# A two-layer hybrid encoder on one core: order of projection units, scan parts and embedding units

## The chip, the cores and the metric

The kernel runs on one core of a Trainium2 chip. A core has a matrix engine (PE, TensorE; PEld is its weight load), a vector engine (DVE, VectorE), a scalar engine (ACT, ScalarE), a third elementwise engine (POOL, GpSimd) and a sequencer that issues transfers (SP, SyncE). They run side by side and meet at semaphores. The metric is the device time of one execution in microseconds (us); lower is better.

## The reference, cut to what matters

Tokens: 512; model width: 1024; two layers; all in float32. A layer, cut from the reference:

```python
u = _rmsnorm(h, norm_mix_g[l])
(s_z, s_xbc, s_dt, g_q, g_f, g_i, g_g, m_q, m_k, m_v, m_i, m_f, m_o,
 gates) = _split(u @ w_in[l], IN_SIZES)
y_ssd = _ssd_branch(s_z, s_xbc, s_dt, ...)        # conv, SSD scan in two directions, gate, group norm
y_hg = _hgrn2_branch(g_q, g_f, g_i, g_g, ...)     # gated linear scan, 8 heads
y_ml = _mlstm_branch(m_q, m_k, m_v, m_i, m_f, m_o, ...)
merged = (gate[:, :, 0] * (y_ssd @ w_br_ssd[l]) + gate[:, :, 1] * (y_hg @ w_br_hg[l])
          + gate[:, :, 2] * (y_ml @ w_br_ml[l]))
h = h + merged @ w_out[l]
u = _rmsnorm(h, norm_ffn_g[l])
up = _dwconv(u @ w_up[l], ffn_conv_w[l], ffn_conv_b[l])
h = h + (jax.nn.silu(a_half) * v_half) @ w_down[l]
h = h + (p[l] @ w_ple[l]) * jax.nn.sigmoid(h @ w_ple_gate[l])
```

A last RMS norm closes the trunk.

## The kernel before, in words

**Units.** Activations lie with channels on the 128 partitions and the 512 tokens along the free axis, so `h` is eight tiles of 128x512. A weight matrix is cut into units of 128 output columns. `weights` (line 192) loads a unit (512 KB, `wraw`) by a transfer on SP's queue and splits it into a rounded high part (`whi`, a cast on ACT) and the rest (`wlo`, a subtraction on DVE); three buffers of each. `proj` (line 214) multiplies: for each of eight slices k of the inner dimension three matmuls (high by high, high by low, low by high) into one PSUM bank. So a unit is 24 matmuls of 512 columns. The four banks of `pbank` are for projections, the four of `bank` for everything else. Nearly every tile of 128x512 comes from one pool with the tag `t2` and 36 buffers (line 1170).

**Norms.** `ssq_add` squares a tile of `h` on ACT and adds it to a running sum on POOL, or on DVE at the program's begin; the last square isn't added, except at the begin. `ssq_end` sums over partitions by small matmuls (`ssq`), `rstd` makes the reciprocal root on DVE and POOL, `ssq_bcast` spreads it by matmuls (`rb`). `norm_split` (line 298) then makes, for each of eight tiles, `u` on DVE, its high part `uh` on ACT and its low part `ul` on DVE. No projection of the next stage can begin before the first `uh`.

**Scans as jobs.** The scans are generators. At each `yield vec, lat` a job says how much DVE time its last part takes and what latency follows; the planner adds that to its own count of DVE time (`self.vec`) and sets the job's `ready`. `tick`, called after each k of a projection, resumes every job whose `ready` has passed in the planner's count of PE time (`self.now`); `finish` resumes without waiting. The planner's numbers only decide the order in which instructions are written down. PE's order is kept in the mixer (`manual_schedule` with PE, line 1005); the other engines' order comes from the framework's scheduler, by priority (`high_priority`).

**The mixer's order.** `ORDER` (line 20) is a list of steps: `a` and `b` are units of the SSD branch's groups 0 and 1 (four `xs`, then `sB`, `sC`), `z` a gate unit, `S` the start of the scalar work `scalars_ssd` (line 308), `0` and `1` the starts of the two SSD scans, `g` and `h` merge-gate units. Behind each `xs` unit `ssd_x` (line 559) makes the five-tap convolution (one ACT operation, four DVE operations) and the activation, giving `xc`, yields, and then has PE transpose `xc` into `tp` (line 189). Then come eight HGRN2 heads. `hg_proj(h)` (line 693) issues the units gq, gf0, gf1, for even heads the value units gv of two heads, and gg; then `finish(hg[h-1])` ends the scan of the head before, and the scan of head h starts. So the scan of an even head lies beside the units of an odd one (gq, gf0, gf1, gg) and the scan of an odd head beside those of an even one, which has the two value units besides. The last part of a head's scan makes the states `hst` and multiplies them into `hpo`; `hg_tail` normalises. `scalars_ml` (line 397) prepares the mLSTM scalars and starts with transposes into `rowp`.

**Begin and norms.** `begin` (line 505) projects the first three units (s0, 64 columns; xs0, xs1) from the tokens before the norm's factor is known, and scales the results afterwards: the s0 unit takes each tile of tokens as it arrives, xs0 and xs1 follow. Behind the norms stand embedding units (`ple_proj`, four pieces of six matmuls each for half of `p[l] @ w_ple[l]`): in layer 0 both halves stand behind the feed-forward norm, layer 1's halves behind the norm at the end of layer 0 and behind its own feed-forward norm. The feed-forward block (`ffn`, line 1093) takes its units `ua`, `uv` in turn.

Of the kernel before, what the change touches and what calls it, by code (L numbers as in the profile page):

```python
# [4 lines left out]
F32 = mybir.dt.float32  # L5
# [14 lines left out]
ORDER = "a a a a a z z a b S z z b 0 b b b b 1 z z z z g g g g g g g g h h h h h h h h"  # L20
# [100 lines left out]
class Body:  # L121
# [81 lines left out]

    def weights_split(self, raw):
# [9 lines left out]
    def proj(self, w, xh, xl, name, c0=0):  # L214
# [4 lines left out]
        for k in range(nk):  # L219
# [4 lines left out]
            if self.jobs:  # L224
                self.tick()
        return ps
# [22 lines left out]
    def ssq_add(self, q, x, later=False):  # L249
# [3 lines left out]
        q["i"] += 1  # L253
        last = q["i"] == q["n"] and not later
# [38 lines left out]

    def norm_apply(self, h, rb, g):
        with self.tc.high_priority(offset=NPRI):
            self.norm_split(h, rb, g)

    def norm_split(self, h, rb, g):
# [3 lines left out]
        for i in range(8):  # L302
            u = self.t2("u")
            nc.vector.scalar_tensor_tensor(u, h[i], self.pc(g, i), rb, op0=ALU.mult, op1=ALU.mult)
            self.split(u, self.uh[i], self.ul[i])


    def scalars_ssd(self):
# [4 lines left out]
        p4 = ps[:, 0:256].rearrange("p (t c) -> p t c", t=4)  # L313
        for t in range(4):
            nc.tensor.transpose(p4[:, t, :], raw[:, t * C:t * C + C], self.c("ident")[0:64, 0:64])
        rw = lambda n: self.rowt[:, ROW[n][0]:ROW[n][0] + ROW[n][1]].unsqueeze(1).to_broadcast([128, 4, ROW[n][1]])
        x = sm.tile([128, 4, 48], F32, name="spx")
        ii = sm.tile([128, 4, 16], F32, name="ii")
        nc.vector.tensor_tensor(x[:, :, 0:32], p4[:, :, 0:32], rw("dtb"), op=ALU.add)
        nc.vector.tensor_tensor(ii, p4[:, :, 32:48], rw("ib"), op=ALU.add)  # L320
        nc.vector.scalar_tensor_tensor(x[:, :, 32:48], p4[:, :, 48:64], -1.0, rw("fb"),
                                       op0=ALU.mult, op1=ALU.subtract)

        fl = lambda t: t.rearrange("p a b -> p (a b)")
        xf = fl(x)
        e = sm.tile([128, 192], F32, name="spe")
        nc.vector.scalar_tensor_tensor(e, xf, -1.0, xf, op0=ALU.mult, op1=ALU.min)
        nc.scalar.activation(e, e, AF.Exp)
        r = sm.tile([128, 192], F32, name="spr")
        nc.vector.tensor_scalar_add(r, e, 2.0)  # L330
        nc.vector.reciprocal(r, r)
        nc.vector.tensor_tensor(r, r, e, op=ALU.mult)
        q = sm.tile([128, 192], F32, name="spq")
        nc.vector.tensor_tensor(q, r, r, op=ALU.mult)
        nc.vector.tensor_scalar_mul(e, q, 2.0 / 17)
        for n in (15, 13, 11, 9, 7, 5, 3):
            nc.vector.scalar_tensor_tensor(e, e, 2.0 / n, q, op0=ALU.add, op1=ALU.mult)
        nc.vector.scalar_tensor_tensor(e, e, 2.0, r, op0=ALU.add, op1=ALU.mult)
        sp = sm.tile([128, 4, 48], F32, name="sp")
        nc.vector.scalar_tensor_tensor(fl(sp), xf, 0.0, e, op0=ALU.max, op1=ALU.add)  # L340
        self.dt = sp[:, :, 0:32]
        a = sm.tile([128, 32], F32, name="acoef")
        nc.scalar.activation(a, self.rowt[:, ROW["alog"][0]:ROW["alog"][0] + 32], AF.Exp)
        la = sm.tile([128, 4, 48], F32, name="la")
        nc.vector.scalar_tensor_tensor(la[:, :, 0:32], self.dt, -1.0,
                                       a.unsqueeze(1).to_broadcast([128, 4, 32]),
                                       op0=ALU.mult, op1=ALU.mult)
        nc.vector.tensor_scalar_mul(la[:, :, 32:48], sp[:, :, 32:48], -1.0)
# [919 lines left out]
```

## Time and profile before

| | |
|---|---|
| median of three runs | 2979.97 us (2977.85 to 2980.33) |
| the profiled execution | 2980.76 us, of which the span is 2978.9 us |
| PE busy | 2896.2 us, 97% of the span |
| DVE, ACT, POOL busy | 1865.3, 1185.4, 270.6 us |
| mean share of the TensorE clock that was granted | 0.987 |

The page shows PE busy in nearly every slice of the span, and of the transfers a mean of 98 GB/s. The time between the span and the profiled execution's own time, 1.9 us, lies outside the program's instructions. Views used below: the waits (who waited for whom), the stretches (busy time of each engine between two points, with the granted clock, called PEclk, 1.00 being full speed), the timeline (instructions in order of time; in brackets how long the engine had been idle and what ended that), and the groups of instructions.

### The profile page before, as it was taken

The page shows a single profiled execution, that of the slowest core. Times are in us where ns is not written, and L with a number is a line of the kernel's source. Part 1 is how long each engine was busy: PE and PEld are TensorE (multiplying, and loading weights), DVE is VectorE, ACT ScalarE, POOL GpSimd, SP SyncE. Part 2 cuts the span into 40 slices and gives each one's busy share as a digit, 9 for nine tenths or more (in the row PEclk, how much of TensorE's full clock was granted, in tenths as well). Part 3 has the DMA queues.
Part 4 walks back from the last instruction along what each step waited for, and adds up shares of the span by engine and source line. Part 5 has one row for each costly group of instructions (what it writes and reads, how often), then busy time and mean ns, then how long its engine had stood idle before and what let it go on. Part 6 is the DMA issues. An engine that isn't in the chain of part 4 may idle for free. (4 is left out here: it accounts for less than half of the span.)

```text
span 2978.9 us, 40295 instructions
## 1 busy us (share of the span) xinstructions
PE 2896.2 (97%) x15998; PEld 2412.1 (81%) x15998; DVE 1865.3 (63%) x3194; ACT 1185.4 (40%) x2018; POOL 270.6 (9%) x209
## 2 busy tenths in 40 slices
PE   7999999999999999999989999999999999999998
PEld 6777788888888888888867787888888888888887
DVE  6776767776565455546458768668765654555454
ACT  5443544553233343334344425455532323433342
POOL 0132100001100110000101321000010001000001
PEclk9999999999999999999999999999999999999999
DMA  3443222223322333333424331221232224332332
GB/s 129 114 128 115 71 72 78 72 72 110 103 85 85 134 114 99 98 94 102 153 90 124 117 114 60 83 72 64 72 121 92 86 92 135 101 98 96 97 101 95
DMA packets 120459, 293.34 MB, mean 98 GB/s; under 512 B 10608, under 2 KB 43760, under 8 KB 120272
## 3 DMA queue, kind: packets, MB, share of 16 engines
q1 hardware_dynamic: 120272, 290.79, 30.4%
q8 instruction: 125, 2.05, 0.3%
q14 instruction: 62, 0.51, 0.1%
HBM read 277.97 MB, written 12.78 MB: 98 GB/s over the span
## 5 line engine op out<-in xcount | busy, mean ns | idle before, releaser
L236 DVE TENSOR_TENSOR wlo<-wraw,whi 128x1024 fp32r<-128x1024 f32 (+2 forms) x454 | 575.2, 1268 | 483.5 <-ACT whi L235 481.0
L235 ACT CAST whi<-wraw 128x1024 fp32r<-128x1024 f32 (+2 forms) x454 | 472.4, 1041 | 895.8 <-issue 146.3
L155 PE MATMUL ga<-uh,whi 128*128 128x512 f32 x384 | 161.2, 420 | 0.0
L155 PE MATMUL pbr<-yh,whi 128*128 128x512 f32 x384 | 153.7, 400 | 0.0
L155 PE MATMUL ga<-uh,wlo 128*128 128x512 f32 x384 | 151.4, 394 | 0.0
L155 PE MATMUL ga<-ul,whi 128*128 128x512 f32 x384 | 150.9, 393 | 0.0
L155 PE MATMUL pbr<-yh,wlo 128*128 128x512 f32 x384 | 150.9, 393 | 0.0
L155 PE MATMUL pbr<-yl,whi 128*128 128x512 f32 x384 | 150.7, 392 | 0.0
L155 PE MATMUL ua<-uh,whi 128*128 128x512 f32 x352 | 137.4, 390 | 3.6 <-ACT uh L235 3.6
L155 PE MATMUL pdn<-sl,whi 128*128 128x512 f32 x352 | 137.4, 390 | 0.0
L155 PE MATMUL pdn<-sh,wlo 128*128 128x512 f32 x352 | 137.2, 390 | 0.0
L155 PE MATMUL ua<-uh,wlo 128*128 128x512 f32 x352 | 137.1, 390 | 0.0
L155 PE MATMUL uv<-uh,whi 128*128 128x512 f32 x352 | 137.1, 390 | 0.0
L155 PE MATMUL uv<-ul,whi 128*128 128x512 f32 x352 | 137.1, 390 | 0.0
L155 PE MATMUL uv<-uh,wlo 128*128 128x512 f32 x352 | 137.1, 390 | 0.0
L155 PE MATMUL pdn<-sh,whi 128*128 128x512 f32 x352 | 136.8, 391 | 0.0
L155 PE MATMUL ua<-ul,whi 128*128 128x512 f32 x352 | 136.8, 390 | 0.0
L258 POOL TENSOR_TENSOR sq<-sq 128x512 f32<-128x512 f32 x36 | 53.0, 1473 | 899.2 <-issue 767.5
L287 POOL TENSOR_TENSOR rs<-ms,mhalf 128x4 f32<-128x4 f32 x41 | 44.7, 1091 | 917.1 <-DVE ms L285 917.1
L774 ACT COPY hqc<-hQ 128x512 f32<-128x512 f32 x96 | 64.4, 671 | 114.8 <-DVE hQ L785 48.1
L155 PE MATMUL gf<-uh,whi 128*128 128x512 f32 x256 | 104.3, 407 | 0.0
L1107 DVE TENSOR_TENSOR h<-h,pdn 128x512 f32<-128x512 f32 x48 | 33.0, 688 | 111.8 <-PE pdn L155 111.8
(409 smaller groups left out, 7508.0 us busy)
## 6 DMA issues: line engine op xcount, KB each, us to landing
wraw<-wf SPq DMA_DIRECT2D x420, 512.0 KB, 3.6
att<-acd SPq DMA_DIRECT2D x32, 512.0 KB, 7.2
wraw<-wf SPq DMA_DIRECT2D x32, 448.0 KB, 3.3
me<-rtd SPq DMA_DIRECT2D x32, 256.0 KB, 4.3
h<-xT SPq DMA_DIRECT2D x16, 256.0 KB, 4.6
gad<-gth SPq DMA_DIRECT2D x16, 256.0 KB, 2.0
gdr<-gad SPq DMA_DIRECT2D x16, 256.0 KB, 5.4
ppd<-pp SPq DMA_DIRECT2D x16, 256.0 KB, 2.1
```

The lines of the kernel that those rows point to most:

```text
L155: return self.nc.tensor.matmul(out, lhsT, rhs, **k)
L235: nc.scalar.copy(hi, src)
L236: nc.vector.tensor_tensor(lo, src, hi.bitcast(F32), op=ALU.subtract)
L258: q["add"].tensor_tensor(q["acc"], q["acc"], sq, op=ALU.add)
L287: self.nc.gpsimd.tensor_tensor(r, ms, self.mhalf.to_broadcast([128, 4]), op=ALU.pow)
L774: nc.scalar.copy(v3(qc), qv)
L1107: nc.vector.tensor_tensor(h[i], h[i], ps, op=ALU.add)
```

## The change

1. **The s0 unit** gets its high and low parts side by side in one 128-column weight tile (`weights_wide`), so that each slice k takes two matmuls and not three; the two halves of the result are added afterwards, behind 128-wide transposes, by a copy and an add on DVE.
2. **The begin**: the first two tiles of tokens are issued from ACT's queue and the weights of s0 and xs0 ahead of the other tiles; s0 and xs0 both take each arriving tile; squares are added on POOL; the first half of layer 0's embedding units stands where the norm is made; then xs2 and xs3 are projected together, slice by slice (`pair_proj`).
3. **Norms**: `norm_split`'s DVE order is written out, `u` one tile ahead of the split. Behind `wo` and behind `pg` PE's order is written out too, and the norm becomes a job (`norm_job`) whose matmuls are placed among the embedding units. The first units of the feed-forward block go slice by slice together. The next layer's parameters are loaded before the norm.
4. **Scan parts later**: `S` moves ahead by five steps of `ORDER`, its yields grow, the transposes of `xc` are planned 6.5 us and not 4.2 us after the DVE work, the planner starts the mixer with 10 us of DVE work, `scalars_ml` waits 4 us before it starts. The convolution's ACT operation gets a high priority.
5. **HGRN2**: the query unit of each next even head (`hg_q`) is issued beside the even head's scan, where until now it stood beside the odd head's; the last one takes mLSTM's first query unit (`ml_q`), and mLSTM's second query and key units surround the end of the last scan.

The diff, cut:

```diff
-ORDER = "a a a a a z z a b S z z b 0 b b b b 1 z z z z g g g g g g g g h h h h h h h h"
+ORDER = "a a a a S z z a a z b z b 0 b b b b 1 z z z z g g g g g g g g h h h h h h h h"
+    def weights_wide(self, raw):
+        raw, nk = raw
+        n = raw.shape[1] // nk
+        w = self.wp.tile([128, 2 * n * nk], F32R, name="whi", tag="whi", padded_shape=[128, 1024])
+        w = w.rearrange("p (k c) -> p k c", k=nk)
+        self.split(raw.rearrange("p (k c) -> p k c", k=nk), w[:, :, 0:n], w[:, :, n:2 * n])
+        return w, None
+    def pair_proj(self, names):
+        ps, w = [self.pbank(n) for n in names], [self.weights(n) for n in names]
+        for k in range(8):
+            self.first_proj(ps, w, k, self.uh[k], self.ul[k])
+            self.tick()
+        return ps
+        if q["i"] == q["n"] and later and not q["whole"]:
+            return sq
+    def norm_job(self, ssq, last, wait, then):
+        yield wait
+        self.ssq_end(ssq, last)
+        r = self.rstd(ssq["ps"][:, 0:4], 1.0 / D, EPS)
+        yield 200, 1700
+        then(self.ssq_bcast(r))
...
-        for i in range(8):
+        def scaled(i):
             u = self.t2("u")
             nc.vector.scalar_tensor_tensor(u, h[i], self.pc(g, i), rb, op0=ALU.mult, op1=ALU.mult)
-            self.split(u, self.uh[i], self.ul[i])
+            return u
+        with self.tc.manual_schedule(engines={mybir.EngineType.DVE}):
+            u = scaled(0)
+            for i in range(8):
+                n = scaled(i + 1) if i < 7 else None
+                self.split(u, self.uh[i], self.ul[i])
+                u = n
...
-            nc.tensor.transpose(p4[:, t, :], raw[:, t * C:t * C + C], self.c("ident")[0:64, 0:64])
+            nc.tensor.transpose(pw[:, t, :], raw[:, t * C:t * C + C], self.c("ident"))
+        p4 = self.t2("spp", 256).rearrange("p (t c) -> p t c", t=4)
+        nc.vector.tensor_copy(p4, pw[:, :, 64:128])
+        nc.vector.tensor_tensor(p4, p4, pw[:, :, 0:64], op=ALU.add)
+        with self.tc.high_priority(offset=WPRI):
...
-        yield 7500, 1500
+        yield 12000, 6000
...
+        yield 0, 4000
         for d in range(2):
             rows = []
...
-        yield 2500, 2500
+        yield 2500, 5000
...
-        nc.scalar.activation(acc, ps, AF.Identity, bias=self.pc("cb", i), scale=w(2))
+        with self.tc.high_priority(offset=WPRI):
+            nc.scalar.activation(acc, ps, AF.Identity, bias=self.pc("cb", i), scale=w(2))
...
             self.mm(p, wh[:, k, :], xh, start=k == 0, stop=False)
+            if wl is None:
+                self.mm(p, wh[:, k, :], xl, start=False, stop=k == 7)
+                continue
...
+            load(0, nc.scalar)
+            load(1, nc.scalar)
             nc.sync.dma_start(g0, self.par[0, :, o:o + 8])
+            raw = [self.weights_load(n) for n in FIRST[:2]]
+            for i in range(2, 5):
+                load(i, nc.sync)
...
-            ssq = self.ssq(8, nc.vector, lambda n: self.tx(n, tag="xd"), whole=True)
+            ssq = self.ssq(8, temp=lambda n: self.tx(n, tag="xd"), whole=True)
-            w.append(self.weights_split(raw[0]))
+            w.append(self.weights_wide(raw[0]))
             for i in range(8):
                 self.split(self.h[i], *x[i], scale=g0[:, i:i + 1])
                 first(i, 0)
-                self.ssq_add(ssq, self.h[i])
+                if i == 1:
+                    w.append(self.weights_split(raw[1]))
+                    first(0, 1)
+                if i:
+                    first(i, 1)
+                    self.ssq_add(ssq, self.h[i - 1])
             w.append(self.weights_split(raw[2]))
+            self.ssq_add(ssq, self.h[7], later=True)
+            for i in range(3):
+                first(i, 2)
+            self.ssq_end(ssq)
+            r = self.rstd(ssq["ps"][:, 0:4], 1.0 / D, EPS)
+            pt = self.ple_split(pt)
+            w.append(self.weights_split(raw[3]))
+            for i in range(3, 8):
+                first(i, 2)
+            rb = self.ssq_bcast(r)
...
+            self.ple_proj(0, 0, pt, w[3])
...
+            if g == 0 and self.l == 0 and i == 2:
+                first = [None] * 2 + self.pair_proj(("xs2", "xs3"))
-        yield 3300 if g else 2600, 4200
+        yield 3300 if g else 2600, 6500
...
+        self.vec = self.now + 10000
+            q = None
             for h in range(8):
-                p = self.hg_proj(h)
+                p = self.hg_proj(h, q or self.hg_q(h))
+                q = (self.hg_q(h + 1) if h < 7 else self.ml_q(0)) if h % 2 else None
...
-            self.ml_first = self.ml_proj(0)
+            ml_first = self.ml_proj(0, q, self.ml_k(0))
+            mq = [self.ml_q(1)]
             self.finish(hg[-1])
+            mq.append(self.ml_k(1))
             for j in self.tails:
                 self.finish(j)
...
+        with self.tc.manual_schedule(engines={mybir.EngineType.PE}):
+            for i in range(8):
...
+                sq = self.ssq_add(ssq, t, later=True)
+            job = self.start(self.norm_job(ssq, sq, (700, 1000), lambda rb: self.norm_apply(self.h, rb, "ffg")))
+            self.ple_proj(self.l, 1, pt)
+            self.finish(job)
-        if self.l == 0:
-            self.ple_proj(self.l, 0, pt)
...
+                pa, pv = self.pair_proj((f"ua{j}", f"uv{j}")) if j == 0 else (self.uproj(f"ua{j}"), None)
...
+                self.layer_params(self.l + 1)
+                job = self.start(self.norm_job(ssq, sq, (1500, 1700), lambda rb: self.norm_apply(self.h, rb, "mix")))
+                self.ple_proj(self.l + 1, 0, pt)
+            else:
+                job = self.start(self.norm_job(ssq, sq, (1500, 1700), self.final))
+            self.finish(job)
```

`first_proj` holds the matmuls of one slice for each of the given units; `ssq_add(..., later=True)` now hands the last square back for `ssq_end`. `ml_q` and `ml_k` are the query and key parts of the old `ml_proj`, `hg_q` the query part of the old `hg_proj`. Layer 1's first three units run under PE's written order too.

More of the change, by code (lines that the diff above doesn't have):

```diff
@@ L320, in scalars_ssd @@
[L320 to L347, printed above, removed]
@@ L495, in first_banks @@
     def first_banks(self):
-        return [self.pbank("s0")[0:64, :], self.pbank("xs0"), self.pbank("xs1")]
+        return [self.pbank("s0"), self.pbank("xs0"), self.pbank("xs1")]
     def first_proj(self, ps, w, k, xh, xl):
@@ L1110, in ple_load, with ple_raw, ple_split @@
     def ple_load(self, l):
+        return self.ple_split(self.ple_raw(l))
+    def ple_raw(self, l):
+        raw = [self.t2("pt") for _ in range(2)]
+        for i, t in enumerate(raw):
+            self.nc.sync.dma_start(t, self.pT[l, i * C:i * C + C, :])
+        return raw
+    def ple_split(self, raw):
         ph, pl = [], []
[L1113 to L1115 removed]
+        for i, t in enumerate(raw):
             ph.append(self.t2("ph", dt=F32R))
@@ L1119, in ple_load, with ple_proj @@
         return ph, pl
-    def ple_proj(self, l, half, p):
-        w = self.weights(f"pl{half}", l)
-        for i in range(4):
+    def ple_proj(self, l, half, p, w=None, tiles=range(4)):
+        w = w or self.weights(f"pl{half}", l)
+        for i in tiles:
             t = self.t2("pp")
@@ L1137, in ple, with final @@
             pt = self.ple_load(self.l + 1)
-        for i in range(8):
-            pp = self.t2("ppr")
-            nc.sync.dma_start(pp, self.ppd[self.l, i])
-            th = self.t2("pth")
-            nc.scalar.activation(th, self.proj(f"pg{i}", hh, hl, "ppg"), AF.Tanh, scale=0.5)
-            nc.vector.scalar_tensor_tensor(th, th, 1.0, pp, op0=ALU.add, op1=ALU.mult)
-            nc.vector.scalar_tensor_tensor(h[i], th, 0.5, h[i], op0=ALU.mult, op1=ALU.add)
-            self.ssq_add(ssq, h[i])
-            if self.l < L - 1:
-                nc.sync.dma_start(self.hd[i * C:i * C + C, :], h[i])
-        rb = self.ssq_rows(ssq, 1.0 / D, EPS)
-        if self.l < L - 1:
-            self.ple_proj(self.l + 1, 0, pt)
-        return rb
+        with self.tc.manual_schedule(engines={mybir.EngineType.PE}):
+            for i in range(8):
+                pp = self.t2("ppr")
+                nc.sync.dma_start(pp, self.ppd[self.l, i])
+                th = self.t2("pth")
+                nc.scalar.activation(th, self.proj(f"pg{i}", hh, hl, "ppg"), AF.Tanh, scale=0.5)
+                nc.vector.scalar_tensor_tensor(th, th, 1.0, pp, op0=ALU.add, op1=ALU.mult)
+                nc.vector.scalar_tensor_tensor(h[i], th, 0.5, h[i], op0=ALU.mult, op1=ALU.add)
+                sq = self.ssq_add(ssq, h[i], later=True)
+                if self.l < L - 1:
+                    nc.sync.dma_start(self.hd[i * C:i * C + C, :], h[i])
+            if self.l < L - 1:
+                self.layer_params(self.l + 1)
[4 more added lines that the diff above has]
+            self.finish(job)
+    def final(self, rb):
+        for i in range(8):
+            o = self.t2("o")
+            self.nc.vector.scalar_tensor_tensor(o, self.h[i], self.pc("fin", i), rb, op0=ALU.mult, op1=ALU.mult)
+            self.nc.sync.dma_start(self.out[i * C:i * C + C, :], o)
     def setup(self, cp):
         nc = self.nc
-        self.cont = cp.tile([128, NCON], F32, name="cont")
-        nc.sync.dma_start(self.cont[:, 0:C], self.con[:, 0:C])
         self.ones = cp.tile([128, 128], F32, name="ones")
@@ L1187, in run @@
                 self.l = l
[L1188 to L1195 removed]
+                if l == 0:
+                    self.norm_apply(self.h, rb, "mix")
+                else:
+                    with tc.manual_schedule(engines={mybir.EngineType.PE}):
+                        ps = self.first_banks()
+                        with tc.high_priority(offset=WPRI):
+                            w = [self.weights_wide(self.weights_load(FIRST[0]))]
+                        w += [self.weights(n) for n in FIRST[1:]]
+                        for k in range(8):
+                            self.first_proj(ps, w, k, self.uh[k], self.ul[k])
+                    self.s0r = self.t2("s0r")
                     nc.scalar.copy(self.s0r, ps[0])
[L1197 to L1199 removed]
+                    first = ps[1:]
+                self.mixer(first)
                 self.ffn()
[L1201 to L1205 removed]
+                self.ple()
 def _layout(inputs):
```

140 lines of the change are left out of this document (73 added, 67 removed).

## The prediction

> **What bounds the kernel now.** First the page's busy times, then who kept PE waiting, then the stretches round those waits with the granted clock.
>
> ```profile
> PE 2896.2 (97%) x15998; PEld 2412.1 (81%) x15998; DVE 1865.3 (63%) x3194; ACT 1185.4 (40%) x2018; POOL 270.6 (9%) x209
> ```
>
> PE is the bound: of the span of 2978.9 us it is idle for 82.7. No other engine is near. So an edit gains only where PE stands still, runs at a lower clock, or has a matmul less. The waits of PE, longest first (line waited for: us in all, times, longest):
>
> ```profile
> PE hpo L155 <- DVE hst L819: 17.3, 6, 3.1
> PE tp L189 <- ACT xc L493: 10.7, 5, 5.1
> PE s L155 <- ACT xh L238: 8.7, 2, 7.3
> PE tp L189 <- DVE xc L491: 8.2, 2, 4.5
> PE rowp L410 <- DVE sz L674: 4.4, 2, 2.2
> PE ua L155 <- ACT uh L235: 3.6, 2, 1.8
> PE cum L155 <- DVE la L348: 3.1, 2, 1.6
> PE rb L155 <- POOL rs L287: 2.7, 4, 1.3
> ...
> PE tp L189 <- ACT hon L848: 1.9, 2, 0.9
> ```
>
> Nearly all of these are waits that the change names. The stretches show what follows them (columns: stretch, its length, busy us of PE, PEld, DVE, ACT, POOL, PEclk, DMA share, GB/s):
>
> ```profile
> 0.00:55.00 55.00, 39.88 (x147) 29.48 (x148) 38.33 (x57) 27.64 (x42) 2.07 (x5) 0.88 0.43 146
> 90.00:150.00 60.00, 52.95 (x229) 41.64 (x229) 50.20 (x101) 29.36 (x61) 8.40 (x8) 0.94 0.42 115
> 315.00:330.00 15.00, 12.80 (x97) 11.98 (x97) 12.22 (x18) 5.22 (x10) 2.97 (x2) 0.89 0.01 1
> 360.00:372.00 12.00, 9.05 (x59) 7.73 (x58) 10.33 (x21) 6.44 (x21) 0.00 (x0) 1.00 0.24 85
> 560.00:572.00 12.00, 9.29 (x51) 8.38 (x50) 8.94 (x17) 5.89 (x19) 1.32 (x1) 0.86 0.15 46
> 640.00:650.00 10.00, 7.28 (x49) 6.47 (x48) 8.35 (x18) 5.56 (x17) 1.10 (x1) 1.00 0.26 82
> 1125.00:1200.00 75.00, 75.00 (x332) 61.87 (x332) 40.23 (x47) 26.04 (x32) 0.00 (x0) 1.00 0.31 95
> 1484.00:1550.00 66.00, 57.38 (x253) 43.85 (x252) 37.17 (x48) 29.30 (x53) 1.02 (x1) 0.95 0.26 87
> 1575.00:1630.00 55.00, 48.85 (x219) 38.41 (x218) 45.83 (x93) 26.05 (x53) 9.19 (x9) 0.97 0.45 121
> 1840.00:1853.00 13.00, 9.87 (x46) 8.72 (x45) 9.38 (x18) 5.97 (x19) 1.39 (x1) 0.74 0.13 41
> 2040.00:2052.00 12.00, 8.86 (x47) 7.83 (x46) 8.93 (x18) 5.71 (x17) 1.20 (x1) 0.86 0.14 46
> 2120.00:2133.00 13.00, 9.85 (x47) 8.66 (x47) 9.39 (x19) 5.98 (x19) 1.33 (x1) 0.74 0.25 66
> ```
>
> The seventh row is the yardstick: 332 matmuls in 75 us without a gap, 0.226 us each; a unit of 24 takes 5.4 us. A PEclk of 0.86 over 12 us is a loss of 1.7 us beside the idle time (as far as the slow part isn't itself idle). What the half clock costs a matmul stands in the begin:
>
> ```profile
> 7.29 0.69 PE L155 MATMUL s<-xh,whi 128*64 128x512 f32 x1 [7.29 <-ACT xh L238]
> ...
> 47.14 1.12 PE L189 MATMUL tp<-cont,xc 128*128 128x128 f32 x4 [5.10 <-ACT xc L493]
> ...
> 50.19 0.63 PE L155 MATMUL xs<-uh,wlo 128*128 128x512 f32 x1
> 50.62 0.63 PE L155 MATMUL xs<-uh,whi 128*128 128x512 f32 x1
> ...
> 54.88 0.40 PE L155 MATMUL sB<-uh,whi 128*128 128x512 f32 x1
> ```
>
> Behind a gap of 5.10 us the matmuls start 0.43 us apart.
>
> **The change part by part.**
>
> *HGRN2.* Six waits for `hst`, all at scans of even heads, which lie beside four units (21.6 us); odd heads' scans have two value units besides, as many columns as two units more (32.5 us), and none waits. An even scan so needs about 21.6 + 2.7 to 3.1 = 24.7 us of cover. The change gives each five (27.1).
>
> ```profile
> L236 DVE TENSOR_TENSOR wlo<-wraw,whi 128x1024 fp32r<-128x1024 f32 (+2 forms) x454 | 575.2, 1268 | 483.5 <-ACT whi L235 481.0
> ```
>
> What the moved unit adds to the chain is one more `wlo` and `whi` on DVE and ACT; a `wlo` costs 1.3, the scan then needs 26.0, still below 27.1. What is removed: idle 2.95, 2.71, 2.72, 3.13, 3.14, 3.15 in the six stretches, 17.8; clock 0.14x12 + 0.26x13 + 0.14x12 + 0.26x13 = 10.1, of which about 1 lies in the idle time. 26.9 at most, 17 if odd scans begin to wait by 1.2 each (eight of them, 10); I take **24**.
>
> [...]
>
> *The two tails behind the last head* (`hon`, 1.9) get a unit of cover: **1.9**, bounds 0 and 2.5.
>
> *Convolution transposes in the SSD stage.* In 90:150 and 1575:1630 PE is idle for 7.05 and 6.15, of it 8.2 for `xc` and 3.1 for `la`, and the clock costs 0.06x60 + 0.03x55 = 5.2, about a third of it inside idle time. `la` is planned 18 and not 9 us ahead of `cum`, with `S` five steps earlier: **3** of 3.1. The transposes come 2.3 us later; unless `xc` itself moves, 2.2 of 4.5 remains. But the scalar chain's DVE work no longer lies just ahead (DVE is busy for 50.2 of 60 there), and gaps of 2 us mostly leave the clock alone. Of 8.2 + 1.2 (second transposes behind it, an estimate from the idle time left) + 3.6 = 13 I take **10**, bounds 4 and 13.4.
>
> *`rowp`.* 4 us of units between the norm's DVE work and the transposes: idle 4.4 and clock 0.11x15 = 1.6. **5**, bounds 3 and 7.
>
> *Feed-forward norms.*
>
> ```profile
> 1064.39 0.28 PE L155 MATMUL ssq<-zero,ones 128*128 128x4 f32 x2
> ...
> 1080.90 0.51 PE L155 MATMUL ua<-uh,whi 128*128 128x512 f32 x1 [1.79 <-ACT uh L235]
> ...
> 2547.90 0.28 PE L155 MATMUL ssq<-zero,ones 128*128 128x4 f32 x2
> ...
> 2558.97 0.51 PE L155 MATMUL ua<-uh,whi 128*128 128x512 f32 x1 [1.79 <-ACT uh L235]
> ```
>
> From the sum to the first `ua`: 16.5 us in layer 0 with 48 embedding matmuls, 11.1 in layer 1 with 24, and the same gap of 1.79 in both. The second half hid nothing: moving it to the begin takes **5.4** from here (what it costs there is in the begin's sum). Of the gaps, 0.30 + 1.79 in each layer, the written order of `u` and the interleaved job can save 4.2 in all; a `wlo` that gets in ahead of `u` costs 1.3 each time. **3**, bounds -2.6 and 4.2.
>
> *Layer 1's begin*, 1484:1550: idle 8.6, clock 0.05x66 = 3.3 (a third of it idle), and 8 matmuls fewer, 1.8. Still there: `u` and `uh` behind `rb`, about 0.7 each, and a wait for xs2's weight split, whose buffer comes free only with s0: 2 to 3 together. The four waits for `xc` here, 10.7 - 5.1 = 5.6 in all, should go: the planner now puts the first transposes 10 + 2.6 + 6.5 = 19.1 us behind the first units, where the code had 2.6 + 4.2. **9.5**, bounds 5 and 12.
>
> *Layer 0's begin.* Prices:
>
> ```profile
> 8.28 0.61 ACT L252 ACTIVATE sq<-h 128x512 f32<-128x512 f32 x1
> 8.80 0.71 ACT L238 ACTIVATE xh<-h,g 128x512 fp32r<-128x512 f32 x1
> ...
> 26.92 2.05 DVE L304 SCALAR_TENSOR_TENSOR u<-h,part,rb 128x512 f32<-128x512 f32 x3
> 28.89 1.28 DVE L236 TENSOR_TENSOR ul<-u,uh 128x512 fp32r<-128x512 f32 x2
> ...
> 104.16 1.04 POOL L630 TENSOR_TENSOR xdt<-xt,dtf 128x512 f32<-128x512 f32 x1
> ...
> 104.17 1.11 DVE L365 TENSOR_TENSOR dac<-ac 128x64 f32<-128x64 f32 x1
> ```
>
> ACT needs 0.71 + 0.61 = 1.32 a token tile, PE five matmuls, 2.1 at half clock and 1.1 at full. The last two rows: a 64-column DVE operation that begins with a POOL operation lasts until that ends. Squares are now added on POOL, so a tile may take a POOL add (1.04 for that size in the last row but one) and the DVE split (0.7, as `u`) one after the other, 1.8. At a mean of 1.6 from a first matmul at 6 (an estimate: 1.3 earlier, as the first tile no longer stands behind other transfers on SP's queue), plus a weight split of 1.3, s0 and xs0 end at 20; xs1 with the sums at 26.5; `rb` at 27.5; 24 embedding matmuls at 33; xs2 and xs3, 48 matmuls, at 43.8. DVE's norm, 8 x (0.68 + 0.64) from 27.5 with two `wlo` and three scalings (4.5), ends at 42.6 and doesn't come later. Until now these four units end at 54.9, or 53.9 without the two groups of transposes that move behind. Then 53.9 - 43.8 = 10; PE's waits for a free bank among the embedding pieces (four banks, three held by the first units) take about 1. **9**, bounds 5 (embeddings not hidden, clock low again) and 12.
>
> [...]
>
> *At nothing:* two more DVE operations of 256 columns in the s0 chain, now five steps ahead of need; wider transposes; the final norm, whose chain at the end is the same.
>
> **Sum:** 24 + 1.9 + 3 + 10 + 5 + 5.4 + 3 + 9.5 + 9 = 70.8. For small waits that appear elsewhere as the order shifts I take off 3: 68. The profiled execution took 2980.8, 0.8 above the median: 2980 - 68 = **2912**.
>
> **Rivals.**
>
> 1. *DVE keeps the waits.* In the SSD stage DVE is 84% busy (50.2 of 60); if `xc` and `la` end where DVE's queue lets them, later parts only wait elsewhere. For it: the transposes wait for DVE's `xc`, not for PE's order. Against: units of PE work stand ready to fill. The terms 10, 3 and 5 fall away: 2930.
> 2. *The query unit moves the wait.* If a scan's chain, with weights split beside it, needs above 27.1 us, all sixteen scans wait, odd ones too, whose cover falls from 32.5. For it: DVE is 8.9 of 12 busy at such a wait. At 1.5 us each 24 are spent and the term is gone: 2936.
> 3. *Tiles run out; slower.* The pool `t2` has 36 buffers. At the last head merged gates (8), finished heads (16) and a scan's own (about 9) hold 33; the change adds a query tile, and two query and two key tiles at the end. From the 37th tile on, ACT's copy out of PSUM waits for a buffer, PE for a bank. To end above the time before it must cost over 74 us: 1.0 us at each of the 72 units of both layers' HGRN2 and first mLSTM heads. Against: 37 is reached at most at that end. About 2990.
> 4. *It doesn't do what it says:* the other engines' order is the scheduler's, which may put the parameter-dependent operations in ACT's way or `wlo` ahead of the norm. Then begins and norms (9, 9.5, 3) give half: 2923.
>
> **How the numbers follow.** Forecast 0.62 (its own range by its terms' bounds: 2892 to 2942); rival 4 0.15, rival 1 0.10, rival 2 0.07, rival 3 0.04, and 0.02 for no change. Best bounds together save 27 + 2.5 + 3.1 + 13.4 + 7 + 5.4 + 4.2 + 12 + 12 = 87, worst 17 + 0 + 0 + 4 + 3 + 5.4 - 2.6 + 5 + 5 = 37. So 2892 to 2943. A measurement here tells 0.2%, 6 us, from no change. Faster 0.94, within 0.2% 0.02, slower 0.04.
>
> **What would show it.** Right: no wait of `hpo` for `hst`; PEclk 1.00 through the HGRN2 heads; first `sB` or `z` matmul near 44; `ua` 11 us behind the sum in both layers; no wait of `tp` for `xc` above 1 us in layer 1. Wrong: waits for `xc` of the old size in the SSD stage, `hpo` waits at odd heads, PEclk below 1 beyond 20 us, PE waiting for ACT copies at the end of the heads.

## Result, and the profile after

The changed kernel takes 2909.49 us (median; 2908.8 to 2912.81), the kernel before 2980.15 us beside it: a ratio of 0.9764, 95% interval 0.9747 to 0.9781, or 65 to 75 us less. The forecast was 2912.

Busy times of the changed kernel, and then the waits of PE, longest first (line waited for: us in all, times, longest):

```profile
PE 2866.8 (99%) x15982; PEld 2393.4 (82%) x15982; DVE 1859.2 (64%) x3193; ACT 1190.8 (41%) x2028; POOL 286.3 (10%) x216
```

```profile
PE s L155 <- DVE whi L253: 8.9, 1, 8.9
PE tp L189 <- DVE xc L530: 5.7, 2, 3.0
...
PE s L155 <- ACT uh L252: 2.6, 1, 2.6
PE xs L155 <- ACT uh L252: 1.9, 1, 1.9
```

The span is 2907.5 us, so PE is idle for 40.7 us where it was 82.7. PE's busy time fell too, by 29.4 us, and the 16 matmuls that the wide s0 units of the two layers save are 3.6 us of that at 0.226 us each. The rest, some 26, I put down to matmuls that no longer run at half clock (in the begin before 0.43 us from one to the next, where 0.226 is usual): the mean granted clock rose from 0.987 to 0.996, and 0.013 of 2979 us less 0.004 of 2907 us is 27. `hpo`, `rowp`, `cum` and `hon` no longer stand among the waits; `xc` does, twice.

The stretches that answer to those of before (stretch, length, busy us of PE, PEld, DVE, ACT, POOL, PEclk, DMA share, GB/s):

```profile
0.00:55.00 55.00, 42.49 (x170) 33.15 (x171) 37.73 (x46) 30.99 (x47) 13.20 (x12) 0.97 0.50 177
...
300.00:315.00 15.00, 15.00 (x126) 14.35 (x125) 10.70 (x14) 8.46 (x15) 2.46 (x3) 1.00 0.13 39
345.00:357.00 12.00, 11.77 (x66) 9.86 (x66) 9.46 (x19) 6.36 (x13) 0.00 (x0) 1.00 0.26 86
```

The last two are `rowp` and an even head's scan: no idle time worth the name, full clock. To see where the gain lies, I cut both programs at the first matmul of s in layer 1, of gq and of `pwo`. Before, and then after:

```profile
1495.44:1765.95 270.51, 256.56 (x1150) 201.18 (x1151) 188.25 (x343) 108.83 (x210) 50.10 (x43) 0.97 0.36 112
288.70:1020.36 731.66, 719.68 (x4774) 614.97 (x4772) 479.79 (x920) 299.58 (x560) 58.93 (x44) 1.00 0.26 85
1765.95:2503.86 737.91, 724.69 (x4773) 619.39 (x4772) 491.61 (x951) 299.57 (x560) 64.34 (x44) 0.99 0.26 84
```

```profile
1462.53:1718.07 255.54, 248.47 (x1143) 198.15 (x1143) 180.97 (x343) 111.86 (x213) 50.69 (x43) 0.99 0.40 118
277.33:994.34 717.01, 716.20 (x4773) 612.02 (x4772) 482.08 (x923) 300.19 (x562) 58.47 (x44) 1.00 0.27 86
1718.07:2434.24 716.17, 715.78 (x4774) 612.18 (x4772) 494.47 (x954) 300.21 (x562) 67.90 (x44) 1.00 0.27 87
```

The first row of each is layer 1's begin and SSD stage, the other two are the heads of both layers. The first gq stands at the left edge of the second row, 288.70 and 277.33, which gives layer 0's begin and SSD stage. For the feed-forward norms, from `pwo` to `ua`, the trace after has these rows:

```profile
1040.42 0.28 PE L155 MATMUL ssq<-zero,ones 128*128 128x4 f32 x2
...
1047.04 0.50 PE L155 MATMUL ua<-uh,whi 128*128 128x512 f32 x1
```

```profile
2480.32 0.28 PE L155 MATMUL ssq<-zero,ones 128*128 128x4 f32 x2
...
2486.94 0.50 PE L155 MATMUL ua<-uh,whi 128*128 128x512 f32 x1
```

So the stages gained: layer 0's begin and SSD stage 11.4 us, the heads 14.7 and 21.7, layer 1's begin and SSD stage 15.0, the norms 7.8 (1020.36 to 1080.90 before, 994.34 to 1047.04 now) and 2.4; together 73.0, of which 1.6 was lost in the rest of the span (71.4 in all).

One trace stands for each kernel, and a stage's length varies between executions of the same instructions. In e1 below the order of PE's matmuls is that of the kernel before until 364 us, and yet its first gq stands at 284.78, 3.9 earlier. In e13, the changed kernel again, it stands at 277.12, the first z at 49.60 (51.54 here), and layer 1's begin and SSD stage takes 257.11. So a difference of less than some 4 us in layer 0's first stage, or 2 in the heads and in layer 1's, shows little by itself. From `pwo` to `ua` kernels with the same norm agree within 0.1.

### The profile page after: what moved, and what is told of

Same layout as the page of the kernel before. It is cut to its first block, busy times and chain, and to the rows that moved or that the text cites. A ratio compares the mean times of both kernels' runs of the same rounds, so it can differ in the third digit from the quotient of the medians.

```text
span 2907.5 us, 40266 instructions
## 1 busy us (share of the span) xinstructions
PE 2866.8 (99%) x15982; PEld 2393.4 (82%) x15982; DVE 1859.2 (64%) x3193; ACT 1190.8 (41%) x2028; POOL 286.3 (10%) x216
## 4 chain that ended last, share of the span: by engine, by line
PE 93%; DVE 3%; DMA 2%; issue 1%; ACT 1%; POOL 1%; SPq 0%; POOLq 0%; DVEq 0%; ACTq 0%
PE pbr L155 9%; PE pdn L155 8%; PE ua L155 8%; PE uv L155 8%; PE ga L155 8%; PE gf L155 6%; PE gv L155 3%; PE mv L155 3%; PE gq L155 3%; PE mo L155 3%; PE z L155 3%; PE mk L155 3%; PE mq L155 3%; PE ppg L155 3%; PE pwo L155 3%; PE gg L155 3%
## 5 line engine op out<-in xcount | busy, mean ns | idle before, releaser
L253 DVE TENSOR_TENSOR wlo<-wraw,whi 128x1024 fp32r<-128x1024 f32 (+1 forms) x452 | 574.2, 1271 | 422.0 <-ACT whi L252 416.4
L277 POOL TENSOR_TENSOR sq<-sq 128x512 f32<-128x512 f32 x43 | 63.1, 1467 | 902.0 <-issue 758.9
```

Of the source, the lines that this page charges most:

```text
L253: nc.vector.tensor_tensor(lo, src, hi.bitcast(F32), op=ALU.subtract)
L277: q["add"].tensor_tensor(q["acc"], q["acc"], sq, op=ALU.add)
```

## The experiments

Each ratio is to the kernel before on the same chip.

### e1: the query units alone

```diff
...
-                p = self.hg_proj(h)
+                p = self.hg_proj(h, q or self.hg_q(h))
+                q = (self.hg_q(h + 1) if h < 7 else self.ml_q(0)) if h % 2 else None
...
```

> The kernel before with part 5 of the change alone: the query unit of the next even head, and at the end mLSTM's first units, beside the even heads' scans. Theory (idle time and half clock at the six waits for hst are PE time lost for want of cover): all six waits go, PEclk is 1.00 at the heads in both layers, and with the two tails about 28 us are saved: 2952 us. Rival (the waits went because scan parts were planned later, or the chain needs more than five units): at least half the waits stay or come back at odd heads, 2965 us or more.

Measured: 2948.93 us, ratio 0.9892 [0.9878, 0.9907], 32 us. The two stretches of the heads:

```profile
284.78:1005.31 720.53, 717.63 (x4774) 613.61 (x4772) 481.21 (x920) 299.03 (x560) 60.03 (x44) 1.00 0.27 86
1752.22:2471.73 719.51, 717.31 (x4773) 613.87 (x4772) 493.74 (x951) 298.91 (x560) 69.63 (x44) 1.00 0.27 86
```

Against 731.66 and 737.91 they gain 11.1 and 18.4, 29.5 in all. That is the upper bound of the forecast's two terms (26.9 and 2.5), and no odd head began to wait: no `hpo` stands among its waits of PE. The theory held, with 32 us for its 28.

### e2: the later parts alone

```diff
-ORDER = "a a a a a z z a b S z z b 0 ...
+ORDER = "a a a a S z z a a z b z b 0 ...
...
-        yield 7500, 1500
+        yield 12000, 6000
...
+        yield 0, 4000
...
-        yield 2500, 2500
+        yield 2500, 5000
...
+        with self.tc.high_priority(offset=WPRI):
...
-        yield 3300 if g else 2600, 4200
+        yield 3300 if g else 2600, 6500
...
+        self.vec = self.now + 10000
...
```

> The kernel before with part 4 alone: S five steps earlier, longer yields, the mixer's 10 us of planned DVE work, priority of the convolution's ACT operation and of the s0 chain. Theory (PE fills the time with units that stand ready): the waits for la and for rowp go (3 and about 7 us with the clock), the four waits for xc in layer 1's begin go (7), those for xc in the SSD stage shrink by half or more (8): about 25 us saved, 2955 us. Rival (DVE sets when xc is done and keeps the waits): only rowp's and la's go, 2970 us.

Measured: 2944.83 us, 0.9878 [0.9861, 0.9894], 36 us: the theory held, and its 25 us were too few. No run separates `S`, the longer yields and the priorities.

```profile
273.92:1003.83 729.91, 720.03 (x4774) 614.75 (x4772) 480.50 (x923) 301.04 (x562) 57.51 (x44) 1.00 0.26 85
1479.00:1734.94 255.94, 251.60 (x1150) 199.24 (x1151) 180.28 (x341) 111.21 (x212) 52.45 (x43) 0.99 0.39 118
```

Layer 1's begin and SSD stage takes 255.94 us, as in the whole change (255.54), though this kernel has none of the edits of the begins. In layer 0 the first gq comes at 273.92, earlier than in the whole change, which however has 24 embedding matmuls ahead of it. The heads, where the waits for `rowp` lie, gain 1.8 and 4.4.

### e3: begins, norms and embeddings alone

The changed kernel with the edits of e1 and e2 undone.

> The changed kernel with the scan parts and the queries put back where they were: only the edits of the two begins, of the norms and of the embeddings are left. Theory (those edits bring the rest of the 71): 3 to 7 below the kernel before, 2974 to 2978, most of it at the first feed-forward norm (6.6 in the trace of the changed kernel). Rival (the terms of the sum on record, 9 + 9.5 + 5.4 + 3): some 27 below, about 2954. Second rival: without the later parts the begin collides with the scan parts that still come early, and the time is at or above that of before.

Measured: 2981.29 us, 0.9993 [0.9984, 1.0002], no difference that can be told: the second rival. Its waits of PE and its stretches:

```profile
PE tp L189 <- ACT xc L529: 11.6, 6, 4.8
...
PE tp L189 <- DVE xc L527: 7.7, 4, 3.6
PE cum L155 <- DVE la L384: 5.6, 2, 2.8
```

```profile
295.30:1028.78 733.48, 721.49 (x4773) 616.36 (x4772) 480.04 (x920) 299.73 (x560) 58.96 (x44) 0.99 0.26 85
```

```profile
1497.01:1768.11 271.10, 255.48 (x1143) 201.92 (x1143) 189.37 (x345) 109.83 (x211) 50.01 (x43) 0.97 0.37 111
```

Layer 1's begin and SSD stage takes 271.10, no less than before, with eight matmuls fewer: the waits for `xc` and `la` are all there, and that for `la` rose from 3.1 to 5.6. In layer 0 the first gq comes 6.6 later than in the kernel before and 10.5 later than in e1, of which the embedding half is 5.4. The norms gain here what they gain in the whole change (from `pwo` to `ua` 52.7 in both layers, before 60.5 and 55.1), and layer 0's first stage loses it.

### e2b, e13 and e14: both together, and the whole beside them

e2b is the kernel before with e1 and e2.

> The kernel before with the later scan parts and the HGRN2 query move, without the three edits of the begin, the norms and the embeddings. Theory (the two gains are in different waits and add): 32 + 36 = 68 below the kernel before, about 2913, so that the begin, the norms and the embeddings bring the whole change only some 4. Rival (the terms of the sum on record): 24 + 1.9 + 5 + 3 + 10 less 3, some 41 below, about 2940, with the other 27 in the edits left out here. Second rival: the two gains share a cause (the clock falls once for either) and the pair gives clearly less than 68, 2920 or more.

Measured: 2914.56 us, 0.9767 [0.9753, 0.9782], 69 us: the two gains add. e13 is the changed kernel again, e14 is e2b again, both on one chip:

> The changed kernel once more, beside the next one on the same chip, to measure what the begins, norms and embeddings are worth on top of the later parts and the query move. Theory (their gain shows only once the later parts have taken the larger waits away): 4 to 7 below the kernel with the later parts and the queries alone, ratio about 0.976. Rival (they are worth nothing, as without the later parts): within 2 of it.

> The kernel with the later parts and the query move alone, once more beside the changed one. Theory: 4 to 7 above the changed kernel, ratio about 0.978. Rival: within 2 of it, ratio 0.9765.

Measured: e13 2910.54 us (2905.5 to 2910.99), 0.975 [0.973, 0.9769]; e14 2914.78 us (2914.17 to 2916.29), 0.977 [0.9751, 0.9789]. The intervals of the ratios overlap, the runs' own ranges don't: the begins, norms and embeddings are worth about 4 us on top of the other two, as the theory had it. The rows of e14 say where.

```profile
1466.56:1722.02 255.46, 251.60 (x1151) 199.28 (x1152) 179.81 (x341) 111.14 (x212) 52.28 (x43) 0.99 0.40 118
272.89:989.84 716.95, 716.13 (x4773) 612.12 (x4772) 481.94 (x923) 300.23 (x562) 58.46 (x44) 1.00 0.28 86
```

```profile
1050.41 0.50 PE L155 MATMUL ua<-uh,whi 128*128 128x512 f32 x1 [1.79 <-ACT uh L235]
```

From `pwo` to `ua` in layer 0 e14 takes 60.6 us, the changed kernel 52.7: 7.9 gained. But layer 0's first gq is at 272.89 here and at 277.33 there: 4.4 of it is lost again in layer 0's begin and SSD stage (2.9 between the other pair, e2b with 274.24 and e13 with 277.12). Layer 1's begin gains nothing: 255.46 and 253.94 (e2b) without the edits, 255.54 and 257.11 (e13) with them.

### e6: the embedding half put back

The first embedding half of layer 0 behind the feed-forward norm again, all else as changed.

> The changed kernel with the first half of layer 0's embedding units back behind layer 0's feed-forward norm. Theory (they fill time at the begin in which PE would stand idle, and hide nothing behind the feed-forward norm): xs2's start at the begin moves forward by 0 to 1 us only, the feed-forward norm of layer 0 is 5.4 us longer, in all 4.5 to 5.4 us slower, 2914. Rival (the begin got longer by the embeddings, as its small gain of 2 us suggests): what is lost at the feed-forward norm is won at the begin, within 1.5 us of the changed kernel.

Measured: 2923.14 us, 0.9807 [0.9793, 0.9821]: some 13 above the changed kernel, much more than either theory. Nearly all of it, 12.9, lies between `pwo` and `ua` (65.6 us; 52.7 in the changed kernel, 60.5 in the kernel before with the same 48 matmuls). The trace has a wait there that neither the kernel before nor the changed one has, and two more in the begin:

```profile
PE ppl L155 <- ACT pp L1205: 6.1, 1, 6.1
PE xs L155 <- ACT uh L252: 3.2, 1, 3.2
PE sB L155 <- DVE cacc L523: 2.9, 1, 2.9
```

With both halves among the norm's matmuls ACT copies the pieces out behind the norm's `uh`, and PE runs out of banks for the next piece. So the new norm needs the embeddings moved; the move isn't worth 13 by itself: e14, below e6 with 0.977, has neither the move nor the new norm. The begin bears the first half of the theory out. Without the 5.4 us of embeddings the first z comes at 47.99 (51.54 in the changed kernel, 49.60 in e13), but the first gq at 279.15, no earlier: PE waits instead, 3.2 for `uh` (1.9 there) and 2.9 for a bank ahead of sB. So as far as one trace tells, what this stage loses against e14 is not the embeddings' own time but lies in the other edits of the begin.

### e4: the constants last on SP's queue

Why did layer 0's begin not come earlier? First its start in the changed kernel (SPq and ACTq issue transfers):

```profile
0.74 0.39 SPq L603 DMA_DIRECT2D cont<-con  x1
...
8.91 0.76 PE L155 MATMUL s<-xh,whi 128*128 128x512 f32 x1 [8.91 <-DVE whi L253]
```

Line 603 is the last of `begin` in the code, but first on the queue: it stands outside the block that writes SP's order, so the scheduler places it. In the kernel before the same line, outside the block too, was issued at 10.14; why it comes first now isn't shown. Before, the first matmul was at 7.29.

```diff
             self.layer_params(0)
+            nc.sync.dma_start(self.cont[:, C:], self.con[:, C:])
...
-        nc.sync.dma_start(self.cont[:, C:], self.con[:, C:])
         return out[1:], rb
```

> The changed kernel with one load moved: the 0.6 MB of constants that its trace shows issued first of all on SP's queue (at 0.74 us, ahead of tokens and weights) now come last in the begin, as in the kernel before. Theory (that load holds up the first token tile and the s0 weights, so that the first matmul comes at 8.9 and not at 7): the first matmul comes about 1.5 to 2 us earlier and the whole is 1 to 2 us shorter, about 2908. Rival (the begin's length is set further on, where the norm's first uh is made, and the earlier start is lost in waits there): within 0.5 us of the changed kernel.

Measured: 2907.68 us, 0.9756 [0.9741, 0.9771]; the first matmul at 6.75. With the constants first it stands at 8.2 to 9.2 (the changed kernel, e3, e6, e13), with them last at 6.2 to 6.9 (e4, e9, e10, e12, e15): that part of the theory is shown. The span is 2905.2, 2.3 below the changed kernel's; the times don't tell the two apart.

### e9, e10, e12, e15: the rest of layer 0's begin

Where the norm follows, the changed kernel's ACT, DVE and PE, one after the other:

```profile
31.67 0.59 ACT L1208 COPY pp<-ppl 128x512 f32<-128x512 f32 x1 [0.81 <-PE ppl L155]
...
36.30 1.04 ACT L252 CAST whi<-wraw 128x1024 fp32r<-128x1024 f32 x1 [0.55 <-PE ppl L155]
...
37.73 1.14 ACT L252 CAST uh<-u 128x512 fp32r<-128x512 f32 x2
```

```profile
33.17 1.41 DVE L331 SCALAR_TENSOR_TENSOR u<-h,part,rb 128x512 f32<-128x512 f32 x2
37.38 1.23 DVE L253 TENSOR_TENSOR wlo<-wraw,whi 128x1024 fp32r<-128x1024 f32 x1 [2.80 <-ACT whi L252]
```

```profile
38.40 0.50 PE L155 MATMUL xs<-uh,whi 128*128 128x512 f32 x1 [1.91 <-ACT uh L252]
```

`u` is there at 33.9, but `uh` is cast at 37.73: ACT's written order puts it behind four copies that wait for PE's embedding matmuls, and the scheduler adds a `whi`. DVE's `ul`, at 38.52, then stands behind the `wlo` of that weight. PE waits 1.91, and the clock over the 12 us from 36 on is 0.86.

e9: as e4, with all four copies out of ACT's written order.

> As e4, with the first embedding unit of layer 0 taken out of the order that is written for all engines: it keeps its place on PE, but ScalarE casts the norm's uh tiles before it copies the pieces out. Theory (the first unit behind the embeddings, xs2, starts late because uh stands behind the four copies): its first matmul comes 1.5 to 2 us after the last embedding matmul less, the 1.91 us gap goes and the half clock behind it with it, 3 to 5 below e4, about 2904. Rival (the rate of u and ul on VectorE sets the start, or the copies come late and hold the embeddings' banks): within 1 of e4, or 1 to 3 above it.

Measured: 2911.32 us, 0.9756 [0.974, 0.9773]. The rival held: no gain over e4, as ACT now made seven `uh` first and PE waited for a bank.

```profile
PE ppl L155 <- ACT pp L1207: 5.8, 1, 5.8
```

e10: as e9, and the second group's transposes later.

```diff
-        yield 3300 if g else 2600, 6500
+        yield (3300, 9500) if g else (2600, 6500)
```

> As e9, with the second group's transposes given a later due time too (9500 instead of 6500). Theory (the waits of 2.68 and 2.98 us of the transposes for xc, and the stretches of half clock behind them, are what is left of the same cause, a due time too short by what VectorE has queued): both waits fall under 1 us, 2 x (2.8 + 1.7) = 9 below e9, about 2895. Rival (the scan of the second group then waits for its xt, or VectorE does the convolution later by as much): within 2 of e9, with the wait named for another tile.

Measured: 2915.31 us, 0.977 [0.9755, 0.9784]. Both waits for `xc` went, as the theory had it, but the scan then waited for its own (8.0; 3.1 in e9), which is the rival's mechanism. The rival's size, within 2 of e9, was too small: the span is 6.7 above e9's (2915.3 and 2908.6). The scan's wait:

```profile
PE py L155 <- DVE att L703: 8.0, 3, 3.6
```

Here a later due time only exchanged one wait for another.

e12: both begins mended (the constants last as in e4; two copies ahead of `uh`, two behind; in layer 1 the last weight split behind the second `ul`, and xs1's first matmuls behind the second slice of s0 and xs0).

```diff
-            self.ple_proj(0, 0, pt, w[3])
+            self.ple_proj(0, 0, pt, w[3], range(2))
...
                     self.norm_apply(self.h, rb, "mix")
+                    with tc.manual_schedule(engines={mybir.EngineType.PE}):
+                        self.ple_proj(0, 0, pt, w0, range(2, 4))
...
                 self.split(u, self.uh[i], self.ul[i])
                 u = n
+                if i == 1 and beside:
+                    beside()
```

> The changed kernel with both begins mended where the traces put their waits: the 0.6 MB of constants last on SP's queue (as e4); the last two of the four embedding pieces of layer 0 copied out behind the norm's uh tiles, the first two ahead of them (e9 had all four behind and PE then waited 5.8 for their banks); in layer 1 the split of xs1's weights put behind the second ul in VectorE's written order, and xs1's first two matmul groups behind the second of s0 and xs0. Theory (what is left of the begins is a gap of 1.9 to 2.6 us with half clock behind it in each): layer 0's first z at 46 to 48 (51.5 in the changed kernel), the gap ahead of layer 1's first s 1.4 or less instead of 2.59 and the clock 1.00 behind it; 2 + 3 + 4 = 9 below the changed kernel, about 2900. Rival (the rate at which VectorE and ScalarE make u, uh and ul sets the begin, and removed gaps come back between the first groups): 2 to 3 below, as e4.

Measured: 2912.16 us, 0.9761 [0.974, 0.9781], no better than the changed kernel. In layer 1 the gap ahead of s fell from 2.59 to 1.49, nearly as the theory had it, but the clock behind it fell all the same (0.86 over 1461 to 1473), and the stage took 257.59, no less than in the changed kernel. In layer 0 the first z came at 45.08, earlier even than the theory's 46, and most of that was lost in the next stretch: 16.7 us from there to sB (11.8 in the changed kernel), where the clock is 0.72 over 57 to 69. ACT, DVE and PE there:

```profile
56.14 0.63 ACT L534 ACTIVATE xc<-cacc 128x512 f32<-128x512 f32 x1 [3.30 <-DVE cacc L525]
56.68 0.76 ACT L521 ACTIVATE cacc<-xs,part 128x512 f32<-128x512 f32 x1
```

```profile
57.48 1.53 DVE L525 SCALAR_TENSOR_TENSOR cacc<-xs,part,cacc 128x510 f32<-128x510 f32 x2 [1.43 <-ACT cacc L521]
58.92 1.22 DVE L253 TENSOR_TENSOR wlo<-wraw,whi 128x1024 fp32r<-128x1024 f32 x1
60.06 1.53 DVE L525 SCALAR_TENSOR_TENSOR cacc<-xs,part,cacc 128x511 f32<-128x511 f32 x2
```

```profile
61.73 0.77 PE L155 MATMUL sB<-uh,whi 128*128 128x512 f32 x1 [4.25 <-DVE cacc L525]
```

A convolution's first step on ACT (`cacc`) stands behind the Silu (`xc`) of the convolution before, that waits for DVE's four taps, and DVE in turn waits for the next `cacc`: 5.5 us a convolution (the Silus start at 50.56, 56.14 and 61.68), though DVE's four taps take 3.1. xs2, whose bank PE needs, is the third in that row.

e15: as e12, with xs2 and xs3 first and the four `cacc` one behind the other.

```diff
+            order, first = (2, 3, 0, 1), first + self.pair_proj(("xs2", "xs3"))
+            with self.tc.manual_schedule(engines={mybir.EngineType.Activation}):
+                for i in order:
+                    acc[i] = self.conv_acc(first[i], i)
```

> As e12, with the four convolutions of layer 0's begin in another order: those of xs2 and xs3, which read PSUM banks, ahead of those of xs0 and xs1, which read SBUF copies and hold no bank; ScalarE's four first steps are written one behind the other, no longer each behind the Silu of the one before. Theory (e12's head start at the first z, 6.5 us, was lost in the 4.25 us gap of sB and the half clock behind it, because xs2's bank came free only when three convolutions had gone through ScalarE and VectorE in turn): the gap of sB goes, the start of the group-1 scan parts (first sps) comes at 99 to 101 instead of 105.9, and the whole is 5 to 6 below e12, about 2905, some 4 below the changed kernel. Rival (the stage ends with the scalar chain and the scan, wherever the units stand): first sps is earlier, but the first gq stands at 277 as in e9, e12 and the changed kernel, and the whole is within 2 of e12.

Measured: 2905.08 us (2902.61 to 2906.86), 0.9745 [0.9732, 0.9759]. The theory held: no wait of `sB`, the scan parts of group 1 (`sps`) start at 99.5 (105.9 in e12), and the time is 7 us below e12's. They ran on two chips; by the ratios it is some 5 us, and the intervals overlap. The run has two edits, the order of the units and the four first steps in a row, and doesn't tell which of them does it.

```profile
47.31 2.71 DVE L529 SCALAR_TENSOR_TENSOR cacc<-xs,part,cacc 128x510 f32<-128x510 f32 x4
49.94 1.22 DVE L253 TENSOR_TENSOR wlo<-wraw,whi 128x1024 fp32r<-128x1024 f32 x1
51.08 2.71 DVE L529 SCALAR_TENSOR_TENSOR cacc<-xs,part,cacc 128x511 f32<-128x511 f32 x4
53.71 5.37 DVE L529 SCALAR_TENSOR_TENSOR cacc<-xsr,part,cacc 128x510 f32<-128x510 f32 x8
```

```profile
270.11:987.01 716.90, 716.08 (x4773) 612.00 (x4772) 482.00 (x923) 300.37 (x562) 58.51 (x44) 1.00 0.27 87
```

DVE takes the sixteen taps with one weight split between, the banks are free at 53.8, and the first gq comes at 270.11, 7.2 earlier than in the changed kernel. It is the lowest median of all kernels run, though its interval overlaps the changed kernel's two.

## Why the prediction was right

The total was right by 3 us, and the mechanism of most of it: nearly all the time is gained where PE waited, and over a third of it (26 of 71 us) is clock. That the total came so near is luck. By edit, the forecast and the runs compare so, in us:

| edits | forecast | measured |
|---|---|---|
| query move and tails, 24 + 1.9 | 25.9 | 32 (e1) |
| later parts, 3 + 10 + 5, and 5.6 of layer 1's begin | 23.6 | 36 (e2) |
| begins, norms, embeddings, 9 + 3.9 + 5.4 + 3 | 21.3 | about 4 (e13 beside e14) |

Two groups were too small and one was about five times too large, and the errors cancel. By stage they cancel in part within the rows:

| terms on record | forecast | measured |
|---|---|---|
| query move and tails, 24 + 1.9 | 25.9 | 29.5 (e1) |
| `rowp` | 5 | 6.9 (heads' 36.4 less 29.5) |
| layer 1's begin, and half of the SSD terms, 9.5 + 6.5 | 16.0 | 15.0 |
| layer 0's begin, and the other half, 9 + 6.5 | 15.5 | 11.4 (7.5 against e1's first gq) |
| norms and embedding half, 5.4 + 3 | 8.4 | 10.2 (7.8 + 2.4) |
| unplaced waits | -3 | -1.6 |

**Query move.** Under-sized: 24 was taken between 17 and 26.9 in case odd heads' scans began to wait. They didn't; both the idle time and the clock came back in full. What came back, 29.5 us, is 10 more than the 19.7 of waiting.

**Layer 0's begin: the step that failed.** "xs2 and xs3, 48 matmuls, at 43.8" (measured: 51.5, in e13 49.6). A first matmul at 6 came at 8.91 (e4: the constants ahead on the queue). The pace of the token tiles was forecast well, 1.6 each: the trace after has five tiles in 8.12 us, 1.62 each, beside POOL adds of 1.72 each, where a split begun with no POOL add beside it takes 0.75; the 1.8 that I had estimated, from an add of 1.04 and a split of 0.7 one after the other, is a little high.

```profile
11.39 0.75 DVE L256 SCALAR_TENSOR_TENSOR xl<-h,g,xh 128x512 fp32r<-128x512 f32 x1
12.53 8.12 DVE L256 SCALAR_TENSOR_TENSOR xl<-h,g,xh 128x512 fp32r<-128x512 f32 x5 [0.38 <-ACT xh L255]
```

"24 embedding matmuls at 33" ended at 36.5. And the norm's work on DVE and ACT, which I let run beside them from 27.5, stood behind the embeddings' copies. The 9 us were to be the edits' own. The kernel without them (e14) has its first z at 46.65, and with the 5.4 us of embeddings added would stand at 52.1: by that reckoning the edits gained 0.5, and 2.5 by e13. What this stage gained came from the later parts, which took away the wait of 5.10 for `xc` that I had put into the begin's 53.9: with them alone (e2) no wait of PE for ACT's `xc` is left, and the first gq stands at 273.92.

**Layer 1's begin.** The size was right and the cause half right. I counted its four waits for `xc`, 5.6, to the planner's later transposes, which e2 bears out; but the remaining 3.9, for eight matmuls and a shorter norm chain, was not gained: with the begin's edits 255.54, without them 255.46, and the second pair says no better. PE was busy 3.1 less and idle 3.2 more (7.07 against 3.86, length less busy time): the saved matmuls came back as waits, the gap of 2.59 ahead of s (1.9 in e14) among them.

**The later parts** were under-sized by edit: alone they bring 36 us, where their terms (3, 10, 5) and the 5.6 make 24. The wait of 5.10 for `xc` in layer 0's begin is one reason, as the sum held it in another term. Another is that it puts little clock behind gaps of 2 us, which it says "mostly leave the clock alone". Before, of the five gaps of 1.9 to 2.2 us that began at full clock, three gave 0.86 over the 12 us round them (at 321, 1495 and 1540), the one at 2965, with another of 1.35 behind it, gave 0.73, and only the one at 1799 gave 1.00; the five of 1.5 to 1.8 us gave 1.00.

**The rivals.** Rival 1 (DVE keeps the waits) holds for 5.7 us: two waits for `xc` of up to 3.0 stay (before, 4.5 and 3.7 at the like places), and e10 only exchanged them for others. Rival 2 fell: no head waits for `hst`. Rival 3 fell: in the heads PE is idle for 0.8 and 0.4 us. Rival 4 (the scheduler puts other work in ACT's way) was true of both begins: in layer 0 a weight cast stands ahead of `uh`, in layer 1 a `wlo` of 1.23 us, at 1459.94, just ahead of `u`. It cost more there than the half that the rival had, as the begins' edits brought 0.5 to 2.5 of 12.9 us; the norms kept their gain, and the larger terms above made up for it.

**Signs on record.** Right: no `hpo` wait, full clock in the heads. Wrong: first z near 44, no `xc` wait over 1 us in layer 1. And one sign of being wrong was there, "PEclk below 1 beyond 20 us": over 12 us from 36, 110 and 1459 on it is 0.86. `ua` stands 6.6 behind the sum in both layers and not 11, since the sum now stands among the embedding matmuls.

## What to carry to other kernels

In this kernel a gap cost its idle time and often, though not in every execution, a half clock behind it (PEclk 0.86 over 12 us, 1.7 us), and both came back when work was put into the gaps of the heads (29.5 us in e1): the upper bound of the query term was the right one, as the new cover was long enough. A sum can come out right while its terms are wrong: only the runs with one group of edits each showed it. When a stage is started earlier, look at the first shared resource behind it, here a PSUM bank that waited for a chain going back and forth between two engines: e12's 6.5 us at the first z were worth nothing until e15 freed that bank. And an instruction left outside a block with a written order, a transfer above all, can land at its front, as the constants did here.

## What the runs showed of the hardware

The length of a gap did not decide here whether the clock fell. In e15, a stretch with a gap of 2.36 us and one with a gap of 1.49:

```profile
104.00:116.00 12.00, 9.64 (x45) 7.36 (x44) 12.00 (x22) 6.16 (x17) 2.12 (x2) 1.00 0.91 230
1454.00:1466.00 12.00, 10.28 (x41) 7.93 (x40) 11.17 (x17) 6.14 (x10) 0.00 (x0) 0.86 0.21 72
```

The shorter one cost the clock, the longer one didn't. Nor did the matmuls beside a gap decide it. The changed kernel and e13 are the same program, and the stretch in which PE waits 1.91 us for `uh` ahead of xs2 looks so in the one, and then in the other:

```profile
36.00:48.00 12.00, 9.73 (x36) 7.33 (x35) 10.62 (x17) 6.93 (x11) 0.00 (x0) 0.86 0.26 96
```

```profile
36.00:48.00 12.00, 9.73 (x41) 7.81 (x42) 11.12 (x17) 6.74 (x11) 0.00 (x0) 1.00 0.26 90
```

The same gap, between the same matmuls, cost the clock in one execution and not in the other; it makes up 1.4 of the 1.9 us by which their first z differ. With the gap of 2.9 to 3.0 us ahead of the transposes at 1552.8 it is the other way round: PEclk is 1.00 over 1549 to 1561 in the changed kernel and 0.86 in e13. So the clock's part of a gap's price, 0.86 or 1.00 over these 12 us, is known for one execution only. No run here shows what decides between the two.
